# Encoder layer: the recurrence's levels on 64 by 64 blocks, and chain steps spread by their own lengths

## The chip, the cores and the metric

The kernel runs on one core of a Trainium2 chip. The core has five engines that work side by side: TensorE (PE in the profile, with its weight loads PEld), VectorE (DVE), ScalarE (ACT), GpSimd (POOL) and SyncE (SP, which issues most DMAs). The metric is the device time in microseconds (us) of one execution, as a median of several. A kernel is compared with another by that time; a profile is taken of one execution apart.

## The reference

One layer of an encoder is applied, with shared weights, to a batch of 512 tokens and a batch of 256 tokens, 1024 wide. Half of the 16 heads are dilated window attention; the other half are bidirectional HGRN2 heads, a gated linear recurrence. What the change touches is the part inside a chunk of 64 tokens:

```python
A = jnp.cumsum(gc, axis=-2)
diff = A[:, :, :, None, :] - A[:, :, None, :, :]
decay = jnp.exp(jnp.where(causal[:, :, None], diff, -jnp.inf))
att = jnp.einsum('bhtk,bhtsk,bhsk->bhts', qc, decay, kc)
o_intra = jnp.einsum('bhts,bhsv->bhtv', att, vc)
```

There is one scan forward and one backward, their outputs are added, normalised and gated, joined with the attention's output, and multiplied by an output weight. A gated feed-forward network with a short convolution follows.

## The kernel before

All 768 tokens are held in on-chip memory with the feature on the partitions. Float32 products of the projections are made as three products of rounded parts (`stationary_w`, L338). The first 25 weight tiles belong to the mixer's input projection. `tile_unit` takes such a tile through eight feature blocks `k`; each `k` is six matmuls of 512 and 256 columns, and each of these is one record in the trace.

**The chain.** For each of four pairs of heads, `chain(j)` computes the recurrence. Instead of a sum over tokens one by one, it builds the 128 by 128 matrix of weights between tokens in levels m = 1, 2, 4, 8, 16, 32, 64: at level m, key block and query block are neighbours of m tokens each. For each level a burst of small float32 matmuls multiplies keys by queries that carry the decay to that level's boundary. Then `update_q` (L409) and `update_k` (L397, L401, L403) multiply the decays of the next level in. Level 0 (the diagonal) and the levels 1 to 16 are computed on blocks of 32 by 32 (`small`, L430): 6 chunks, 4 blocks and 2 heads make 48 matmuls a burst. Level 0 is copied to a small array `cd`, and each level is laid over it under a mask (`copy_predicated`, L449), which is 1 where key and query differ by that level. Level 32 is a burst of 24 matmuls of 64 by 64 (L468), the two halves of the 128 by 128 matrix that lie off the diagonal another 24 (L477). Then follow transposes of the keys (L492), products of keys and values (L499), their combination (`comb`, L510), the output (L524, L527), the sums of squares (L534), the reciprocal root on GpSimd (L538), its spreading over 64 columns (L540), transposes of that (L544) and the gating (L546, L547).

**What sets the order.** The chain is a generator: each `yield` ends a step. `tile_unit` calls `pace(0.5)` after each `k`, so that a step of the chain is put in after every two `k` (12 records of L338). In the stretch of value tiles (`value_tile`, L346) after the fourth pair, `side(2)` puts in two steps after each of six tiles; what is left over goes into the tile unit behind. Each unit also splits the weight tile three ahead into its rounded part (ACT, L242) and the rest (DVE or POOL, L243). Within each engine instructions run in order. For TensorE, VectorE and ScalarE this order is laid out by a scheduler when the kernel is built; for SyncE and GpSimd it is the order of the code.

Of the kernel before, what the change touches and what calls it, by code (L numbers as in the profile page):

```python
# [19 lines left out]
NPAIR = 4  # L20
EPS = 1e-6
BRANCHES = ((128, 1), (512, 4), (2048, 16))
LEVELS = (1, 2, 4, 8, 16)
HALF = ((0, 64), (64, 128))


# [27 lines left out]
def const_arrays():  # L54


    c = np.zeros((128, N_CST), np.float32)
    c[:, C_IDENT:C_IDENT + 128] = np.eye(128)
    c[:64, C_ONES] = 1.0
    c[64:, C_ONES + 1] = 1.0  # L60
    tab = np.zeros((128, N_TAB), np.float32)
    p = np.arange(128)[:, None]
    delta = np.abs(p - (np.arange(896)[None, :] - 384))
    mult = np.zeros(delta.shape, np.float64)
    for window, dil in BRANCHES:
        mult += (delta % dil == 0) & (delta // dil <= window // (2 * dil))
    tab[:, :896] = np.where(mult > 0, 8.0 * np.log(np.maximum(mult, 1.0)), -1e30)
    inv = np.float32(500000.0) ** (-np.arange(8, dtype=np.float32) * np.float32(2.0) / np.float32(16))
    pos = np.concatenate([np.arange(SA), np.arange(SB)]).astype(np.float32)
    ang = (pos[None, :] * inv.astype(np.float32)[:, None]).astype(np.float32).astype(np.float64)  # L70
    for row in range(64):
        r = row % 16
        tab[row, 896:896 + T] = np.cos(ang[r % 8])
        tab[64 + row, 896:896 + T] = np.sin(ang[r % 8]) * (-1.0 if r < 8 else 1.0)
    s = np.arange(32)
    x = s[:, None] ^ s[None, :]
    m = np.zeros((128, len(LEVELS), 32), np.int32)
    for i, lv in enumerate(LEVELS):
        m[:, i] = np.tile((x >= lv) & (x < 2 * lv), (4, 1))
    return c, tab, m.reshape(128, -1)  # L80


# [10 lines left out]
class Encoder:  # L93
    def __init__(self, tc, a):
        self.tc, self.nc, self.a = tc, tc.nc, a
        self.pools = {}
        self.open("c", "left")
        self.cst = self.pools["c"][1].tile([128, N_CST], F32, name="cst")
        self.par = self.pools["c"][1].tile([128, NROWS], F32, name="par")
        self.sm = self.pools["c"][1].tile([128, 512], F32, name="sm")  # L100
        self.nsm = 0
        self.ident = self.cst[:, C_IDENT:C_IDENT + 128]
        self.W = self.ref("c", "W", 8192, True)
        self.RAW = self.ref("c", "RAW", 3072)
        self.V = self.ref("c", "V", 6144)
        self.open("x", "right")
        self.X = self.ref("x", "X", 12288, True)
        self.xh, self.xl = self.X, self.X + 6144
        self.open("s", "left")
        S0 = self.ref("s", "S0", 4608)  # L110
        self.open("u", "left")
        self.pm = self.pools["u"][1].tile([128, len(LEVELS), 32], I32, name="pm")
        S = self.S = self.ref("u", "S", 15488)
        n = 0

        def region(k):
            nonlocal n
            n += k
            return S + (n - k)

        self.sets = [(S0, S0 + 1536, S0 + 2304), (region(1536), region(768), region(768))]
        self.G = region(768)
        self.LQ = [S0]
        self.U = region(3072)
        self.KT = region(1024)
        self.Kb = region(768)
        self.ATT = region(1536)
        self.S1, self.S2 = region(768), region(768)
        self.TT = region(1536)
        self.CD = region(384)  # L130
        self.MZ = region(1024)
        self.SQ = region(768)
        self.psum = tc.tile_pool(name="ps", bufs=1, space=bass.MemoryType.PSUM)
        self.ps = self.psum.__enter__().tile([128, 8, 512], F32, name="ps")
# [111 lines left out]
    def prologue_loads(self):  # L246
# [29 lines left out]
        nc.sync.dma_start(self.pm, a["pmask"].rearrange("p (l s) -> p l s", s=32))  # L276
        yield

    def params(self):
# [135 lines left out]
    def chain(self, j):  # L415
# [7 lines left out]
        def small(kt, qv):  # L423
            b = 4 + 2 * par[0]
            par[0] ^= 1
            for c in range(NTT):
                for bk in range(4):
                    t0 = 128 * c + 32 * bk
                    for h in range(2):
                        nc.tensor.matmul(ps[32 * bk:32 * bk + 32, b + h, 32 * c:32 * c + 32], self.v(kt + t0, 32, *HALF[h]),  # L430
                                         qv(t0, h), start=True, stop=True)
            return ps[:, b:b + 2, 0:192].rearrange("p h (c s) -> p h c s", s=32)

        cd = self.v(self.CD, 384).rearrange("p (h c s) -> p h c s", h=2, s=32)
        ts = [(self.U, T)]
        for m in (1, 2, 4, 8, 16, 32, 64):
            ts.append((self.TT if m == 1 else ts[-1][0] + ts[-1][1] * 2, ts[-1][1] // 2))
        kb = [ka, self.Kb]
        s = small(kd, lambda t0, h: self.v(q + t0, 32, *HALF[h]))
        nc.scalar.activation(cd, s, AF.Copy)  # L440
        self.update_k(1, *ts[0], ka, kc, self.Kb)
        self.next_products(*ts[0], ts[1][0])
        yield

        def after(i, m, s=None):

            self.update_q(m, *ts[i], q2)
            if s is not None:
                nc.vector.copy_predicated(cd, self.pm[:, i][:, None, None, :].to_broadcast([128, 2, NTT, 32]), s)  # L449
            if m < 64:  # L450
                self.update_k(2 * m, *ts[i + 1], kb[(i + 1) % 2], kc, kb[i % 2])
                self.next_products(*ts[i + 1], ts[i + 2][0])

        for i, m in enumerate(LEVELS):
            after(i, m, small(kb[i % 2], lambda t0, h: self.q_view(q2, m, t0, 32, h)))
            yield


        def att(c, h, sb, tb):
            o = 128 * (c % 4) + 64 * tb  # L460
            return ps[64 * sb:64 * sb + 64, 4 + 2 * h + c // 4, o:o + 64]

        kt = kb[1]
        for c in range(NTT):
            for cb in range(2):
                t0 = 128 * c + 64 * cb
                for h in range(2):
                    nc.tensor.matmul(att(c, h, cb, cb), self.v(kt + t0, 64, *HALF[h]), self.q_view(q2, 32, t0, 64, h),  # L468
                                     start=True, stop=True)
        after(5, 32)  # L470
        yield
        kt = kb[0]
        for c in range(NTT):
            for cb in range(2):
                s0, t0 = 128 * c + 64 * cb, 128 * c + 64 * (1 - cb)
                for h in range(2):
                    nc.tensor.matmul(att(c, h, cb, 1 - cb), self.v(kt + s0, 64, *HALF[h]),  # L477
                                     self.v(q2 + T * (1 - cb) + t0, 64, *HALF[h]), start=True, stop=True)
        after(6, 64)
        kt = kb[1]  # L480
        t, nb = ts[7]
        for h in range(2):
            for b, n in ((0, SA), (1, SB)):
                nc.scalar.activation(self.v(self.ATT + T * h + SA * b, n), ps[:, 4 + 2 * h + b, 0:n], AF.Copy)
        am = self.v(self.ATT, 2 * T).rearrange("p (h c s) -> p h c s", h=2, s=128)
        for bk in range(4):
            nc.vector.tensor_copy(am[32 * bk:32 * bk + 32, :, :, 32 * bk:32 * bk + 32], cd[32 * bk:32 * bk + 32])
        yield

        src = [kt + 128 * c for c in range(6)] + [kc + 128, kc + 256]  # L490
# [4 lines left out]
        yield  # L495
        tok = [0, 1, 2, 3, 4, 5, 1, 2]
        for n in range(8):
            for h in range(2):
# [16 lines left out]
        comb(7, tb(2), 3, 7)  # L515
        comb(2, tf(2), 6, 2)
        comb(1, tb(1), 7, 1)
        yield
# [12 lines left out]
        yield  # L531
# [7 lines left out]
        yield  # L539
        nc.vector.tensor_copy(self.v(self.SQ, T).rearrange("p (n v) -> p n v", v=64), rs[:, :, None].to_broadcast([128, 12, 64]))  # L540
        yield
# [370 lines left out]
    def run(self):  # L912
# [8 lines left out]
        heavy, light = [], []  # L921

        def side(n=1):
            for _ in range(n):
                while heavy:
                    try:
                        next(heavy[0])
                        break
                    except StopIteration:
                        heavy.pop(0)  # L930

        def finish():
            while heavy:
# [11 lines left out]
        def pace(x):  # L945
            nonlocal due
            due += x
            while due >= 1:
                due -= 1
                side()  # L950


        self.prenorm_rows(0)
# [38 lines left out]
        for j in range(NPAIR):  # L992
# [3 lines left out]
                n += 1  # L996
            finish()
            heavy.append(self.chain(j))

        for i in range(NTT):  # L1000
            out = ps[:, (0, 2, 1, 3)[i % 4], 0:384]
# [232 lines left out]
```

## Time and profile before

| what | value |
|---|---|
| median of 3 runs | 1038.61 us (1038.47 to 1043.16) |
| profiled execution: its own time | 1039.73 us |
| profiled execution: span in the trace | 1037.9 us |
| granted TensorE clock, mean | 0.993 of full speed |
| TensorE busy | 997.8 us, 96% |
| VectorE busy | 641.5 us, 62% |
| ScalarE busy | 496.1 us, 48% |
| matmul records, weight-load records | 8239, 8239 |
| the chains' stretch of the program | about 90 to 310 us |

"Busy" is the time in which an engine has an instruction under way. An engine's idle time is put down to what ended it last: "DVE S L510" says that VectorE's line 510 released it; "issue" says that the engine waited for nothing that the profile shows. Each float32 matmul of the chain is two records of PE and two of PEld. In a row of the timeline, neighbouring instructions are merged, "x96" is their count, and the brackets tell the idle time before the row.

### The profile page before, as it was taken

To read this page: it belongs to the slowest core of one execution; us is meant where nothing else is said; L and a number is where in the kernel's file an instruction comes from. 1 tells how busy PE (TensorE), PEld (TensorE's weight loads), DVE (VectorE), ACT (ScalarE), POOL (GpSimd) and SP (SyncE) were. 2 spreads that over 40 slices of the span, in tenths; PEclk is the share of its full clock that TensorE was granted. 3 is DMA by queue.
4 is the path that set the end of the run, shared out by engine and by line. 5 is a ranking of instruction groups with operands and counts; after the bars stand their busy time and mean duration, and the time that the engine had idled before them with its cause. 6 is when DMAs were issued, how large, how long until landed. Compare 5 with 4: busy or idle time off the path is not lost.

```text
span 1037.9 us, 19821 instructions
## 1 busy us (share of the span) xinstructions
PE 997.8 (96%) x8239; PEld 889.0 (86%) x8239; DVE 641.5 (62%) x1110; ACT 496.1 (48%) x909; POOL 49.5 (5%) x45
## 2 busy tenths in 40 slices
PE   5998999989999999999989999999999999999997
PEld 5987788778878777679879999999999998888885
DVE  5445748375631776736799778877777773335334
ACT  4362526243232888854656555555445563334321
POOL 1100000000012101000100000000000000000001
PEclk9999999999999999999989999999999999999999
DMA  8041111111023221123335322333323376475413
GB/s 273 19 123 42 43 42 44 42 27 39 23 62 93 61 64 42 51 103 115 120 96 146 112 86 83 101 108 112 112 83 101 105 239 214 163 255 171 127 46 122
DMA packets 109883, 104.04 MB, mean 100 GB/s; under 512 B 4602, under 2 KB 89698, under 8 KB 109794
## 3 DMA queue, kind: packets, MB, share of 16 engines
q1 hardware_dynamic: 108930, 101.21, 31.9%
q8 instruction: 64, 1.05, 0.4%
q10 hardware_dynamic: 864, 1.57, 0.4%
q14 instruction: 25, 0.20, 0.1%
HBM read 85.46 MB, written 14.94 MB: 97 GB/s over the span
## 4 chain that ended last, share of the span: by engine, by line
PE 80%; issue 7%; DVE 6%; ACT 3%; DMA 1%; POOL 1%; SPq 0%; DVEq 0%; POOLq 0%; ACTq 0%
PE ps L857 31%; PE ps L1159 17%; PE ps L338 17%; PE ps L723 4%; PE ps L643 2%; PE ps L430 2%; PE ps L676 2%; PE ps L346 2%; PE ps L665 2%; PE ps L527 1%; DMA RAW<-w_in 1%; DVE S L412 1%; ACT W L242 1%; POOL sm L304 1%; PE ps L524 1%
## 5 line engine op out<-in xcount | busy, mean ns | idle before, releaser
L338 PE MATMUL ps<-X,W 128*128 128x512 f32 (+1 forms) x1200 | 230.4, 342 | 1.3 <-issue 1.3
L338 PEld LDWEIGHTS ps<-X,W 128*128 128x128 f32 x1200 | 185.1, 188 | 28.6 <-issue 3.8
L857 PE MATMUL ps<-XN,W 128*128 128x384 f32 x1056 | 191.7, 339 | 4.7 <-ACT XN L808 4.2
L857 PEld LDWEIGHTS ps<-XN,W 128*128 128x128 f32 x1056 | 186.5, 191 | 6.1 <-ACT XN L808 5.0
L1159 PE MATMUL ps<-W,XN 128*128 128x512 f32 x792 | 179.7, 389 | 0.0
L1159 PEld LDWEIGHTS ps<-W,XN 128*128 128x128 f32 x792 | 148.7, 188 | 30.8
L242 ACT ACTIVATE W<-RAW 128x1024 fp32r<-128x1024 f32 (+1 forms) x92 | 79.6, 868 | 179.5 <-PE ps L338 81.8
L857 PE MATMUL ps<-X,W 128*128 128x384 f32 x792 | 143.2, 338 | 0.0
L857 PEld LDWEIGHTS ps<-X,W 128*128 128x128 f32 x792 | 139.8, 188 | 0.0
L243 DVE TENSOR_TENSOR W<-RAW,W 128x512 fp32r<-128x512 f32 (+1 forms) x82 | 78.1, 955 | 74.6 <-ACT W L242 74.6
L242 ACT ACTIVATE W<-V 128x512 fp32r<-128x512 f32 x88 | 55.2, 629 | 58.6 <-PE ps L857 55.1
L243 DVE TENSOR_TENSOR W<-V,W 128x512 fp32r<-128x512 f32 x88 | 59.7, 687 | 17.8 <-ACT W L242 17.7
L346 PE MATMUL ps<-W,X 128*128 128x256 f32 (+1 forms) x432 | 66.5, 310 | 4.2 <-ACT X L817 2.7
L346 PEld LDWEIGHTS ps<-W,X 128*128 128x128 f32 x432 | 61.4, 194 | 5.9 <-ACT X L817 3.3
L243 DVE TENSOR_TENSOR XN<-X,XN 128x768 fp32r<-128x768 f32 x44 | 41.8, 955 | 35.8 <-ACT XN L242 35.8
L242 ACT ACTIVATE XN<-X 128x768 fp32r<-128x768 f32 x44 | 36.7, 839 | 42.8 <-PE ps L1159 42.1
L723 PE MATMUL ps<-W,X 128*128 128x512 f32 (+1 forms) x288 | 57.1, 343 | 0.0
L723 PEld LDWEIGHTS ps<-W,X 128*128 128x128 f32 x288 | 44.1, 189 | 6.8 <-issue 1.6
L242 ACT ACTIVATE W<-EX 128x512 fp32r<-128x512 f32 (+1 forms) x34 | 25.3, 744 | 46.8 <-PE ps L1159 22.5
L243 DVE TENSOR_TENSOR W<-EX,W 128x512 fp32r<-128x512 f32 (+1 forms) x34 | 28.2, 828 | 29.3 <-ACT W L242 29.3
L304 POOL TENSOR_TENSOR sm<-sm 128x1 f32<-128x1 f32 x24 | 15.2, 641 | 622.8 <-DVE sm L748 588.0
L397 ACT ACTIVATE S<-S 128x384 f32<-128x384 f32 x28 | 15.4, 549 | 46.9 <-PE ps L430 36.6
(187 smaller groups left out, 1159.6 us busy)
## 6 DMA issues: line engine op xcount, KB each, us to landing
X<-gd SPq DMA_DIRECT2D x44, 384.0 KB
RAW<-w_in SPq DMA_DIRECT2D x32, 512.0 KB
RAW<-w_gate SPq DMA_DIRECT2D x14, 512.0 KB
RAW<-w_up SPq DMA_DIRECT2D x13, 512.0 KB
RAW<-w_down SPq DMA_DIRECT2D x13, 512.0 KB
gd<-UM SPq DMA_DIRECT2D x22, 256.0 KB
EX<-w_up SPq DMA_DIRECT2D x9, 512.0 KB
EX<-w_down SPq DMA_DIRECT2D x9, 512.0 KB
```

The lines of the kernel that those rows point to most:

```text
L242: nc.scalar.activation(self.r(hi, n), self.v(src, n), AF.Copy)
L243: (eng or nc.vector).tensor_tensor(self.r(lo, n), self.v(src, n), self.v(hi, n), op=OP.subtract)
L304: self.nc.gpsimd.tensor_tensor(r, mean, self.mhalf, op=OP.pow)
L338: nc.tensor.matmul(out, self.r(wo + 128 * k, 128), self.r(xo + T * k + t0, tn), start=(k == 0 and first), stop=(k == NK - 1 and last))
L346: self.nc.tensor.matmul(out, self.r(xo + T * k + 128 * i, 128), self.rap(wo + 128 * k, [[1024, tiles], [1, 128]]), start=(k == 0 and first ...
L430: nc.tensor.matmul(ps[32 * bk:32 * bk + 32, b + h, 32 * c:32 * c + 32], self.v(kt + t0, 32, *HALF[h]), qv(t0, h), start=True, stop=True)
L643: nc.tensor.matmul(ps[:, 4 + h, 0:L], self.r(QS + T * h + t0 + 128 * i, 128), self.r(x + T * h + t0, L), start=z, stop=not z)
L665: nc.tensor.transpose(ps[:, 6 + h, 128 * kt:128 * kt + 128], ms(j, n, h)[:, 128 * kt:128 * kt + 128], self.ident)
L676: nc.tensor.matmul(o[64 * h:64 * h + 64], self.v(vb + 128 * kt + 64 * h, 64), self.v(pt(s, h) + L * kt, L), start=kt == 0, stop=kt == L // ...
L723: nc.tensor.matmul(out, self.r(mo + T * f + 128 * i, 128), rhs, start=(f == 0 and first), stop=(f == NK - 1 and last))
L857: nc.tensor.matmul(out, self.r(wo + 128 * k, 128), self.r(xo + H * k, H), start=kind in BEGINS and k == 0 and first, stop=k == 3 and last, ...
L1159: nc.tensor.matmul(ps[:, banks[half][i], :], self.r(go + 128 * i, 128), self.r(wo_, 512), start=(f == 0 and first), stop=(f == NF - 1 and ...
```

## The change

The levels 0 to 16 are computed on blocks of 64 keys by 64 queries: 24 matmuls a burst, each with 64 weights' columns and 64 columns streamed. Level 32 becomes the sixth level of the same loop, laid over `cd` by its mask, so `cd` and the mask double in width (`cd` from 384 to 768 columns, the mask from 160 to 384 int32 columns, all loaded from memory at the start). The two off-diagonal halves are written to the same compact layout. The attention matrix is then put together by two copies on ScalarE and two on VectorE instead of four and four.

Each step of the chain now yields a length, and `pace` takes that length off what is due, so that the following step comes sooner or later by it. The steps of the sums of squares and of the spreading are one step. `side(2)` in the value tiles still takes two steps, whatever their lengths. The chain has 13 steps, before 14.

```diff
-LEVELS = (1, 2, 4, 8, 16)
+LEVELS = (1, 2, 4, 8, 16, 32)
...
-        self.pm = self.pools["u"][1].tile([128, len(LEVELS), 32], I32, name="pm")
+        self.pm = self.pools["u"][1].tile([128, len(LEVELS), 64], I32, name="pm")
...
-                for bk in range(4):
-                    t0 = 128 * c + 32 * bk
+                for cb in range(2):
+                    t0 = 128 * c + 64 * cb
                     for h in range(2):
-                        nc.tensor.matmul(ps[32 * bk:32 * bk + 32, b + h, 32 * c:32 * c + 32], self.v(kt + t0, 32, *HALF[h]),
+                        nc.tensor.matmul(ps[64 * cb:64 * cb + 64, b + h, 64 * c:64 * c + 64], self.v(kt + t0, 64, *HALF[h]),
                                          qv(t0, h), start=True, stop=True)
...
-        s = small(kd, lambda t0, h: self.v(q + t0, 32, *HALF[h]))
+        s = small(kd, lambda t0, h: self.v(q + t0, 64, *HALF[h]))
         nc.scalar.activation(cd, s, AF.Copy)
         self.update_k(1, *ts[0], ka, kc, self.Kb)
         self.next_products(*ts[0], ts[1][0])
-        yield
+        yield 1.3
...
         for i, m in enumerate(LEVELS):
-            after(i, m, small(kb[i % 2], lambda t0, h: self.q_view(q2, m, t0, 32, h)))
-            yield
-
-
-        def att(c, h, sb, tb):
-            o = 128 * (c % 4) + 64 * tb
-            return ps[64 * sb:64 * sb + 64, 4 + 2 * h + c // 4, o:o + 64]
-
-        kt = kb[1]
-        for c in range(NTT):
-            for cb in range(2):
-                t0 = 128 * c + 64 * cb
-                for h in range(2):
-                    nc.tensor.matmul(att(c, h, cb, cb), self.v(kt + t0, 64, *HALF[h]), self.q_view(q2, 32, t0, 64, h),
-                                     start=True, stop=True)
-        after(5, 32)
-        yield
+            after(i, m, small(kb[i % 2], lambda t0, h: self.q_view(q2, m, t0, 64, h)))
+            yield 1.25
...
-        for h in range(2):
-            for b, n in ((0, SA), (1, SB)):
-                nc.scalar.activation(self.v(self.ATT + T * h + SA * b, n), ps[:, 4 + 2 * h + b, 0:n], AF.Copy)
         am = self.v(self.ATT, 2 * T).rearrange("p (h c s) -> p h c s", h=2, s=128)
-        for bk in range(4):
-            nc.vector.tensor_copy(am[32 * bk:32 * bk + 32, :, :, 32 * bk:32 * bk + 32], cd[32 * bk:32 * bk + 32])
-        yield
+        s = ps[:, b:b + 2, 0:64 * NTT].rearrange("p h (c s) -> p h c s", s=64)
+        for cb in range(2):
+            p0, p1 = HALF[cb]
+            nc.scalar.activation(am[p0:p1, :, :, 64 - p0:128 - p0], s[p0:p1], AF.Copy)
+            nc.vector.tensor_copy(am[p0:p1, :, :, p0:p1], cd[p0:p1])
+        yield 0.6
...
             while due >= 1:
-                due -= 1
-                side()
+                due -= side()
```

The lengths of the later steps are 1 (transposes), 1.2 (products and combination), 0.7 (output), 2.3 (sums of squares with the spreading) and 1 (the last).

The first place is VectorE in the first chain, at the levels 1, 2 and 4. L409 multiplies the queries, L449 lays the level over `cd`, L401 and L403 multiply the keys, L243 is the remainder of a weight tile's split. Before:

```order
L449 COPY_PREDICATED S<-pm,ps 128x384
L401 TENSOR_TENSOR S_71<-S 128x96x2 x2
L403 TENSOR_TENSOR S_71<-S 128x96x4
L409 TENSOR_TENSOR S_71<-S_71,S 128x192x2x2
L449 COPY_PREDICATED S<-pm,ps 128x384
L401 TENSOR_TENSOR S<-S_71,S 128x48x4 x2
L403 TENSOR_TENSOR S_71<-S_71,S 128x48x8
L243 TENSOR_TENSOR W<-RAW,W 128x1024
L409 TENSOR_TENSOR S_71<-S_71,S 128x96x2x4
```

And of the change:

```order
L449 COPY_PREDICATED S<-pm,ps 128x768
L401 TENSOR_TENSOR S_71<-S 128x96x2 x2
L403 TENSOR_TENSOR S_71<-S 128x96x4
L243 TENSOR_TENSOR W<-RAW,W 128x1024
L409 TENSOR_TENSOR S_71<-S_71,S 128x192x2x2
L449 COPY_PREDICATED S<-pm,ps 128x768
L401 TENSOR_TENSOR S<-S_71,S 128x48x4 x2
L403 TENSOR_TENSOR S_71<-S_71,S 128x48x8
```

The split's remainder now stands ahead of level 2's L409, where it stood ahead of level 4's.

The second place is TensorE at the end of the last chain, in the first tile unit behind the value tiles. L534 (L522 in the change) are the sums of squares, L544 (L531) the transposes that need the spread reciprocal roots. Before, with 20 records of L338 between them:

```order
L534 MATMUL ps<-cst,S 128x2 x4
L338 MATMUL ps<-X,W 128x256
L534 MATMUL ps<-cst,S 128x2 x2
L338 MATMUL ps<-X,W 128x512
...
L338 MATMUL ps<-X,W 128x256
L544 MATMUL ps<-cst,S 128x128 x6
```

And of the change, with 8:

```order
L522 MATMUL ps<-cst,S 128x2 x4
L338 MATMUL ps<-X,W 128x256
L522 MATMUL ps<-cst,S 128x2 x2
L338 MATMUL ps<-X,W 128x512
...
L338 MATMUL ps<-X,W 128x256
L531 MATMUL ps<-cst,S 128x128 x6
```

Twelve records of L338 have moved from ahead of these transposes to behind them.

The third place is VectorE at the end of the first chain, where the next chain's queries are made (L374, L376) and the old chain's output is gated (L546 and L547; L533 and L534 in the change). Before:

```order
L537 TENSOR_SCALAR sm<-ps 128x12
L540 COPY S<-sm 128x768
L243 TENSOR_TENSOR W<-RAW,W 128x1024
L374 TENSOR_TENSOR S<-ps,S 128x512
L374 TENSOR_TENSOR S<-ps,S 128x256
L376 TENSOR_TENSOR S<-S 128x1536
L546 TENSOR_TENSOR S<-ps,S 128x512
L546 TENSOR_TENSOR S<-ps,S 128x256
L547 TENSOR_TENSOR V<-ps,S 128x512
```

And of the change:

```order
L243 TENSOR_TENSOR W<-RAW,W 128x1024
L374 TENSOR_TENSOR S<-ps,S 128x512
L374 TENSOR_TENSOR S<-ps,S 128x256
L412 TENSOR_TENSOR S<-S 128x12
L376 TENSOR_TENSOR S<-S 128x1536
L525 TENSOR_SCALAR sm<-ps 128x12
L527 COPY S<-sm 128x768
L533 TENSOR_TENSOR S<-ps,S 128x512
L533 TENSOR_TENSOR S<-ps,S 128x256
```

The end of the old chain now comes after the next chain's queries. On TensorE its last transposes stand 12 records of L338 ahead of the next chain's first burst, where they stood 36 ahead.

## Rows read from the trace of the kernel before

**Rows 1.** Page, busy time of each engine, its share of the span, instructions.
```profile
PE 997.8 (96%) x8239; PEld 889.0 (86%) x8239; DVE 641.5 (62%) x1110; ACT 496.1 (48%) x909; POOL 49.5 (5%) x45
```

**Rows 2.** Chains' stretch: length, busy PE, PEld, DVE, ACT, POOL; clock; DMA share, GB/s.
```profile
90.00:310.00 220.00, 206.44 (x3830) 174.97 (x3830) 129.87 (x241) 79.52 (x155) 11.41 (x5) 1.00 0.15 40
```

**Rows 3.** Waits of PE, whole span: waiting line, releaser, us in total, times, longest.
```profile
PE ps L430 <- issue: 8.3, 7, 2.0
PE ps L544 <- DVE S L540: 1.7, 1, 1.7
PE ps L527 <- DVE S L510: 1.7, 3, 0.6
PE ps L499 <- ACT S L494: 0.5, 3, 0.2
```

**Rows 4.** Timeline of PE, first chain: start, us, instruction, count, idle before.
```profile
93.84 0.94 PE L430 MATMUL ps<-S 64*32 64x32 f32 x83
96.51 0.30 PE L430 MATMUL ps<-S 64*32 64x32 f32 x13 [1.72 <-issue]
96.74 2.35 PE L338 MATMUL ps<-X,W 128*128 128x512 f32 x12
99.02 1.02 PE L430 MATMUL ps<-S,S 64*32 64x32 f32 x96
99.97 1.31 PE L338 MATMUL ps<-X,W 128*128 128x512 f32 x6
102.59 1.21 PE L338 MATMUL ps<-X,W 128*128 128x512 f32 x6 [1.30 <-issue]
```

**Rows 5.** Sum over the eight idle stretches of PE put down to issue.
```profile
sum 9.64, PE 0.05 PEld 0.01 DVE 1.76 ACT 0.00 POOL 0.00; mean PE 0.01 PEld 0.00 DVE 0.22 ACT 0.00 POOL 0.00
```

**Rows 6.** Page, DMA: all packets; one queue's packets, MB, share of 16 engines.
```profile
DMA packets 109883, 104.04 MB, mean 100 GB/s; under 512 B 4602, under 2 KB 89698, under 8 KB 109794
...
q8 instruction: 64, 1.05, 0.4%
```

**Rows 7.** Lines by form: count, busy us, mean ns, idle before and its releasers.
```profile
L430 PE MATMUL ps<-S 64*32 64x32 f32 x1920 | 21.5, 202 | 6.3 <-issue 6.3
...
L430 PE MATMUL ps<-S,S 64*32 64x32 f32 x384 | 4.4, 200 | 2.0 <-issue 2.0
...
L477 PE MATMUL ps<-S 64*64 64x64 f32 x192 | 3.7, 222 | 0.0
```

**Rows 8.** Timeline of PE, second chain: level 1's burst and the chain's one gap.
```profile
151.48 1.06 PE L430 MATMUL ps<-S 64*32 64x32 f32 x96
...
166.14 0.26 PE L430 MATMUL ps<-S 64*32 64x32 f32 x5 [0.56 <-issue]
```

**Rows 9.** Timeline of DVE, first chain, split and level 4.
```profile
104.57 1.23 DVE L243 TENSOR_TENSOR W<-RAW,W 128x1024 fp32r<-128x1024 f32 x1 [2.05 <-ACT W L242]
105.71 0.95 DVE L409 TENSOR_TENSOR S<-S,S 128x768 f32<-128x768 f32 x1
106.58 0.60 DVE L449 COPY_PREDICATED S<-pm,ps 128x384 f32<-128x384 int32 x1
...
107.59 0.55 DVE L403 TENSOR_TENSOR S<-S 128x384 f32<-128x384 f32 x1
```

**Rows 10.** Timeline of PE, first chain, level 8's burst (its queries come from level 4's L409).
```profile
106.95 1.02 PE L430 MATMUL ps<-S,S 64*32 64x32 f32 x96
```

**Rows 11.** Timeline of PE, end of the last chain.
```profile
301.02 0.50 PE L534 MATMUL ps<-cst,S 128*128 128x2 f32 x4
301.38 3.75 PE L338 MATMUL ps<-X,W 128*128 128x512 f32 x20
306.87 0.88 PE L544 MATMUL ps<-cst,S 128*128 128x128 f32 x6 [1.74 <-DVE S L540]
```

**Rows 12.** Timeline of DVE, end of the last chain.
```profile
304.10 2.71 DVE L540 COPY S<-sm 128x768 f32<-128x768 f32 x1 [2.38 <-POOL sm L538]
...
308.50 1.01 DVE L547 TENSOR_TENSOR V<-ps,S 128x512 f32<-128x512 f32 x2
```

More of the change, by code (lines that the diff above doesn't have):

```diff
@@ L74, in const_arrays @@
         tab[64 + row, 896:896 + T] = np.sin(ang[r % 8]) * (-1.0 if r < 8 else 1.0)
-    s = np.arange(32)
+    s = np.arange(64)
     x = s[:, None] ^ s[None, :]
-    m = np.zeros((128, len(LEVELS), 32), np.int32)
+    m = np.zeros((128, len(LEVELS), 64), np.int32)
     for i, lv in enumerate(LEVELS):
-        m[:, i] = np.tile((x >= lv) & (x < 2 * lv), (4, 1))
+        m[:, i] = np.tile((x >= lv) & (x < 2 * lv), (2, 1))
     return c, tab, m.reshape(128, -1)
@@ L111, in __init__ @@
         self.open("u", "left")
-        self.pm = self.pools["u"][1].tile([128, len(LEVELS), 32], I32, name="pm")
-        S = self.S = self.ref("u", "S", 15488)
+        self.pm = self.pools["u"][1].tile([128, len(LEVELS), 64], I32, name="pm")
+        S = self.S = self.ref("u", "S", 15872)
         n = 0
@@ L129, in __init__ @@
         self.TT = region(1536)
-        self.CD = region(384)
+        self.CD = region(768)
         self.MZ = region(1024)
@@ L275, in prologue_loads @@
         nc.sync.dma_start(self.v(PR, 128, o, o + 3 * NF), a["conv_w"].rearrange("l w (k p) -> (l w k) p", p=128))
-        nc.sync.dma_start(self.pm, a["pmask"].rearrange("p (l s) -> p l s", s=32))
+        nc.sync.dma_start(self.pm, a["pmask"].rearrange("p (l s) -> p l s", s=64))
         yield
@@ L426, in small @@
             for c in range(NTT):
-                for bk in range(4):
-                    t0 = 128 * c + 32 * bk
+                for cb in range(2):
+                    t0 = 128 * c + 64 * cb
                     for h in range(2):
-                        nc.tensor.matmul(ps[32 * bk:32 * bk + 32, b + h, 32 * c:32 * c + 32], self.v(kt + t0, 32, *HALF[h]),
+                        nc.tensor.matmul(ps[64 * cb:64 * cb + 64, b + h, 64 * c:64 * c + 64], self.v(kt + t0, 64, *HALF[h]),
                                          qv(t0, h), start=True, stop=True)
-            return ps[:, b:b + 2, 0:192].rearrange("p h (c s) -> p h c s", s=32)
-        cd = self.v(self.CD, 384).rearrange("p (h c s) -> p h c s", h=2, s=32)
+            return ps[:, b:b + 2, 0:64 * NTT].rearrange("p h (c s) -> p h c s", s=64)
+        cd = self.v(self.CD, 768).rearrange("p (h c s) -> p h c s", h=2, s=64)
         ts = [(self.U, T)]
@@ L448, in after @@
             if s is not None:
-                nc.vector.copy_predicated(cd, self.pm[:, i][:, None, None, :].to_broadcast([128, 2, NTT, 32]), s)
+                nc.vector.copy_predicated(cd, self.pm[:, i][:, None, None, :].to_broadcast([128, 2, NTT, 64]), s)
             if m < 64:
@@ L454, in chain @@
         for i, m in enumerate(LEVELS):
-            after(i, m, small(kb[i % 2], lambda t0, h: self.q_view(q2, m, t0, 32, h)))
-            yield
-        def att(c, h, sb, tb):
-            o = 128 * (c % 4) + 64 * tb
-            return ps[64 * sb:64 * sb + 64, 4 + 2 * h + c // 4, o:o + 64]
-        kt = kb[1]
-        for c in range(NTT):
-            for cb in range(2):
-                t0 = 128 * c + 64 * cb
-                for h in range(2):
-                    nc.tensor.matmul(att(c, h, cb, cb), self.v(kt + t0, 64, *HALF[h]), self.q_view(q2, 32, t0, 64, h),
-                                     start=True, stop=True)
-        after(5, 32)
-        yield
+            after(i, m, small(kb[i % 2], lambda t0, h: self.q_view(q2, m, t0, 64, h)))
+            yield 1.25
+        b = 4 + 2 * par[0]
         kt = kb[0]
@@ L476, in chain @@
                 for h in range(2):
-                    nc.tensor.matmul(att(c, h, cb, 1 - cb), self.v(kt + s0, 64, *HALF[h]),
+                    nc.tensor.matmul(ps[64 * cb:64 * cb + 64, b + h, 64 * c:64 * c + 64], self.v(kt + s0, 64, *HALF[h]),
                                      self.v(q2 + T * (1 - cb) + t0, 64, *HALF[h]), start=True, stop=True)
@@ L494, in chain @@
             nc.scalar.activation(self.v(self.KT + 512 * b, 512), ps[:, 4 + b, :], AF.Copy)
-        yield
+        yield 1
         tok = [0, 1, 2, 3, 4, 5, 1, 2]
@@ L517, in chain @@
         comb(1, tb(1), 7, 1)
-        yield
+        yield 1.2
         inter = [[(0, 1)], [(1, 0), (0, 7)], [(0, 3), (1, 6)], [(1, 2)], [(0, 5)], [(1, 4)]]
@@ L530, in chain @@
         nc.scalar.activation(self.v(self.SQ + SA, SB), o[1], AF.Square)
-        yield
+        yield 0.7
         ss = ps[:, 6, 0:12]
@@ L538, in chain @@
         nc.gpsimd.tensor_tensor(rs, ms, self.mhalf.to_broadcast([128, 12]), op=OP.pow)
-        yield
         nc.vector.tensor_copy(self.v(self.SQ, T).rearrange("p (n v) -> p n v", v=64), rs[:, :, None].to_broadcast([128, 12, 64]))
-        yield
+        yield 2.3
         rb = [ps[:, 7, :], ps[:, 6, 0:256]]
@@ L923, in side @@
         def side(n=1):
+            d = None
             for _ in range(n):
@@ L926, in side @@
                     try:
-                        next(heavy[0])
+                        d = next(heavy[0])
                         break
@@ L930, in side @@
                         heavy.pop(0)
+            return d or 1
         def finish():
@@ L998, in run @@
             heavy.append(self.chain(j))
+            due = 0.0
         for i in range(NTT):
```

## The prediction

> **What bounds the kernel now.** I read the busy shares first: TensorE is busy for 96% of the span, VectorE 62%, ScalarE 48% [rows 1]. So a term counts if it shortens TensorE's work or its idle time, and VectorE's and ScalarE's work counts only where TensorE waits for it. Then I cut the span by stage. In the chains' stretch, 220.00 us long, TensorE is busy 206.44 us, so 13.6 us are idle there, while VectorE works 129.87 us and ScalarE 79.52 us [rows 2]. The change acts here alone; behind this stretch the order of every engine's instructions stays as it was. The granted clock is full in it [rows 2], so it is no term.
>
> The list of TensorE's waits says what the 13.6 us are. The largest is L430, the bursts of 32 by 32, 8.3 us in 7 waits put down to "issue", which means that no semaphore is seen to hold the engine. Beside it stand 1.7 us of L527 for VectorE's combination, 1.7 us of L544 for the spreading and 0.5 us of L499 for ScalarE [rows 3]. With one more "issue" gap just behind a burst, in L338 [rows 4], the issue gaps are eight stretches, 9.64 us together, in which TensorE runs nothing [rows 5].
>
> What are these gaps? In the timeline of the first chain the reader is to count. Between the start of the record row at 96.51, which ends one gap, and the next gap at 101.28, TensorE runs 13 + 12 + 96 + 6 = 127 matmul records [rows 4]. Each has a weight load beside it, so this is 254 instructions. Now the whole program: 8239 matmuls and 8239 weight loads [rows 1] came in 64 packets of a queue of the kind "instruction", 1.05 MB [rows 6], which is 257 instructions and 16.4 KB a packet. So the gaps lie one packet of instructions apart: TensorE has run out of code. In a 32 by 32 stretch it uses 2 x 108 instructions in 3.2 us (one burst and 12 records of L338, 96.74 to 99.97), a packet in 3.8 us. In the stretches with 24 matmuls a burst, a packet lasts twice as long, and L477's matmuls have no idle time ahead of them [rows 7].
>
> The Trainium skill (Runtime: NRT & Kernel Launch, section "Instruction fetch mechanics") says that code comes in blocks of 256 instructions, fetched while the block before is run, and that crossing a boundary is "mostly hidden". This trace agrees in the block, by the 257 above, and not in the hiding, by the 9.64 us. By the rule the gaps would have another cause and stay, which is the first rival below.
>
> **The change part by part.**
>
> Stalls for code. A burst has 48 records of matmul where it had 96; in a chain, 288 records fall away, 1152 in all. The level stretch takes 48 + 15 records, twice, in one burst of about 0.9 us and 15 records of L338 at 0.19 us, so a packet lasts some 7.5 us instead of 3.8. I take 1.2 us of the 9.64 to stay, one gap of the kind seen: -8.4 us. Bounds: 0, if the gaps are not the code, and -9.6.
>
> Shorter bursts. The 24 bursts of L430 are busy 21.5 + 4.4 = 25.9 us, 1.08 us each; four bursts of 64 by 64 in L477 are busy 3.7 us, 0.93 us each [rows 7]. So half as many matmuls with twice the columns take 0.15 us less: 24 x 0.15 = -3.6 us. Level 32 and the off-diagonal bursts are of this form already and stay. What the trace does not show is 64 columns read in runs of 1 to 16 elements, as the levels 1 to 16 read their queries. For 32 columns the worst case, level 1, is drawn with 1.06 us [rows 8] and level 2 with 1.02 [rows 4], both under the mean of 1.08, so I charge nothing for the pattern. Bounds: -3.6, and twice the pass, 0.93 more on each of 20 bursts, +18.6, which is a rival.
>
> The Trainium skill (TensorEngine Tiling (Array Packing), section "Tiling Modes") gives eight independent tiles for 64 rows by 32 columns and four for 64 by 64. By that count a burst of half as many matmuls with twice the columns on half as many tiles would take twice as long. The 0.93 against 1.08 us says otherwise for this shape, so the tiles are not what sets the pace here; the time by the rule is that of the slow bursts below.
>
> Steps spread. The 192 records of L338 in a chain stay the same. Between products and output there are now 18 of them, before 12, so the combination gets 1.1 us more cover; the waits of L527 were 0.6 us at the longest [rows 3], so 1.7 us go. Of the 0.5 us of L499, whose distance stays 12, I take 0.3 to go, as the cross blocks now leave by two ScalarE instructions instead of four. Together -2.0 us; bounds -2.2 and 0.
>
> End of the last chain. Here the lengths do not help: the value tiles take two steps each, and one step less brings the transposes 12 records earlier. Before, 20 records (3.75 us) covered the way from the sums of squares over GpSimd and the 2.71 us copy, and 1.74 us were still idle [rows 11, 12]. Eight records cover 12 x 0.187 = 2.25 us less: +2.25 us. Nothing takes it back, as the copy and what comes before it start at the same point of the program. Bounds: +0.7, if the copy took 1.2 us, twice the masked copy of half its width [rows 9], and +2.25.
>
> VectorE. The masked copy of 384 columns took 0.60 us [rows 9]; 768 columns cost between 0.60 and 1.2, and I take 1.0. A level on VectorE ran from 105.71 to 108.14, 2.4 us [rows 9], and becomes 2.8 us. TensorE's period is 3.2 us with 12 records of L338 between bursts and 4.3 us with 18, so the level fits behind it. It is close in two places. First, the split now stands ahead of level 2's L409, and the next burst is 12 records later. The same pattern was there before at level 4: split from 104.57, L409 done at 106.66, burst at 106.95 [rows 9, 10], 0.29 us to spare. The burst in between is 0.09 to 0.15 us shorter now, so 0.15 to 0.2 us are left; what queues behind the split are that L409 and the level's other updates, and the next burst waits for L409. Second, a new chain's first burst writes the banks which the old chain's L547 reads. From the transposes to the end of L547 it took 306.87 to 309.51 = 2.64 us [rows 11, 12]; the new cover is the transposes and 12 records, 0.88 + 2.25 = 3.1 us at most, before 36 records. I charge 0.8 us for five such crossings. Bounds: 0 and +7.2, which is 0.3 us on each of 24 bursts.
>
> ScalarE's larger copy of level 0 and the two half-width copies are hidden: it works 79.52 of 220 us [rows 2], and no burst waits for them directly. The mask load grows from 80 to 192 KB in the prologue; at the mean of 100 GB/s [rows 6] that is 1.1 us of transfers at most, in a queue with weight tiles behind it, and I take +0.3.
>
> Sum: -8.4 - 3.6 - 2.0 + 2.25 + 0.8 + 0.3 = -10.65 us. From the profiled execution's 1039.73 us (span 1037.9 and 1.8 around it) this gives 1029.1. The median before lies 1.1 us lower, at 1038.61, so I predict **1028.0 us**.
>
> **The rivals.**
>
> The stalls stay. If the fetch is late because of the weight transfers that go at the same time and not because of the rate, or if the gaps are something else that the profile does not see, fewer instructions do little. For it: the second chain has the same rate and one gap of only 0.56 us [rows 8], so rate alone is not the cause. Against it: spacing by packets, and none in the 64 by 64 stretches of four chains. All of them staying gives 1028.0 + 8.4 = 1036.4 us, half of them 1031.6.
>
> VectorE becomes the bound of the levels. If a masked copy from the accumulation banks under a broadcast mask costs more than twice the old one, or the scheduler's order makes a split wait, each of 24 bursts starts some 0.3 us late: 7.2 us, 6.4 over my 0.8, which makes 1034.4 us. Against it: 129.87 of 220 us busy.
>
> The wide bursts read slowly (the other side). With short runs a 64-column burst could need its pass twice, 1.86 us. It is at the levels 1 to 16, 5 x 4 = 20 bursts; price 20 x 0.93 = 18.6 us, so 1046.6 us. It makes the kernel slower than before from 10.6 / 20 = 0.53 us a burst. Against it are level 1's burst in 1.06 us [rows 8] and level 2's in 1.02 [rows 4], where runs of 1 and of 2 cost nothing that can be seen.
>
> **How the numbers follow.** A measurement of this kernel can tell about 0.5%, 5.2 us, from no change: faster is under 1033.4, slower over 1043.8. The forecast has a chance of 0.70, with 1025.0 (all gaps, all waits gone, no new ones) to 1033 as its own range. Stalls staying, 0.16, a third of it on the fast side of 1033.4. VectorE the bound, 0.08, mostly within 0.5%, a quarter faster. Slow bursts, 0.04, slower. The last 0.02 is for what I do not see, slower or same. That is faster 0.77, same 0.18, slower 0.05. The range is from 1024.0 to 1036.0: it takes in the stalls' bound but for its end and VectorE's case, and leaves the slow bursts out.
>
> **What would show it.** Right: bursts of x48 at 0.93 us at all levels; the "instruction" queue at some 55 packets; the issue waits of the bursts down to 2 us or less; L527's counterpart without waits; the last transposes with some 4 us of idle time ahead of them; and 220 us of stage in about 209. Wrong: issue gaps still one packet apart and over 1 us long; bursts of the low levels longer than those of level 32; TensorE idle for L409 or L449 at each level. A change in time behind the chains' stretch would also prove me wrong, since I expect none there.

## The result and the profile after

The changed kernel takes **1028.52 us** (median of 4, 1027.96 to 1028.98); before took 1039.25 beside it. The ratio is 0.9889, 95% interval [0.9863, 0.9915]. Predicted were 1028.0 us. The profiled execution took 1028.98 us with a span of 1027.2.

The page's busy line, and its row of the "instruction" queue (packets, MB, share of 16 engines), answer to [rows 1, 6]:

```profile
PE 996.8 (97%) x7087; PEld 888.9 (87%) x7087; DVE 651.8 (63%) x1106; ACT 498.3 (49%) x901; POOL 49.4 (5%) x45
...
q8 instruction: 55, 0.90, 0.4%
```

Read TensorE's two numbers together: 1152 records are gone, and 9 packets of code, but only 1.0 us of busy time. So of the span's 10.7 us, 9.7 are idle time. (The busy time holds two terms of opposite sign, shorter bursts and matmuls at a slow clock; both come below.) Of TensorE's waits in the chains' stretch [rows 3], this is what the list still shows:

```profile
PE ps L531 <- DVE S L527: 3.8, 1, 3.8
```

The waits of L430 for issue, of L527 for the combination (L515 in the changed kernel) and of L499 for ScalarE (L487) have no row left. All 28 bursts of L430, level 32 now among them, start right behind what stands ahead of them. Here are level 1 and level 2 of the first chain in TensorE's timeline (start, us, count; compare [rows 4]):

```profile
94.39 1.23 PE L430 MATMUL ps<-S 64*64 64x64 f32 x48
95.55 3.43 PE L338 MATMUL ps<-X,W 128*128 128x512 f32 x18
98.91 0.97 PE L430 MATMUL ps<-S,S 64*64 64x64 f32 x48
99.80 2.37 PE L338 MATMUL ps<-X,W 128*128 128x512 f32 x12
102.10 0.93 PE L430 MATMUL ps<-S 64*64 64x64 f32 x48
```

Level 1's burst takes 95.55 - 94.39 = 1.16 us, level 2's 0.89. The masked copy and the place where the split stands ahead of level 2's L409, in VectorE's timeline (answering to [rows 9]):

```profile
99.76 1.23 DVE L243 TENSOR_TENSOR W<-RAW,W 128x1024 fp32r<-128x1024 f32 x1 [0.54 <-ACT W L242]
100.90 0.95 DVE L409 TENSOR_TENSOR S<-S,S 128x768 f32<-128x768 f32 x1
101.77 1.05 DVE L449 COPY_PREDICATED S<-pm,ps 128x768 f32<-128x768 int32 x1
```

L409 is done at 101.85 and the burst that needs it starts at 102.10: 0.25 us to spare, and no wait. The other close place is the second chain's first burst, which has to come behind the old chain's last gating (VectorE's timeline, then TensorE's):

```profile
140.70 1.01 DVE L534 TENSOR_TENSOR V<-ps,S 128x512 f32<-128x512 f32 x2
```

```profile
141.95 0.93 PE L430 MATMUL ps<-S 64*64 64x64 f32 x48
```

The gating ends at 141.71, 0.24 us ahead of the burst, and TensorE has no idle time there.

The one place that got worse is the last chain's end [rows 11]. First TensorE's timeline, then a window (length, busy PE, PEld, DVE, ACT, POOL, granted clock, DMA share, GB/s):

```profile
286.35 1.64 PE L338 MATMUL ps<-X,W 128*128 128x512 f32 x8
291.81 1.54 PE L531 MATMUL ps<-cst,S 128*128 128x128 f32 x6 [3.82 <-DVE S L527]
```

```profile
290.90:297.40 6.50, 5.59 (x19) 4.94 (x20) 2.81 (x5) 0.00 (x0) 0.44 (x1) 0.50 0.28 81
```

The idle time grew from 1.74 to 3.82 us, and at its end and behind it the granted clock is 0.50, the level of 1.2 GHz, for 6.5 us. The transposes are drawn with 1.54 us where they took 0.88, and the L338 behind them runs slowly too. The prediction had the first part and not the second.

### The profile page after: what moved, and what is told of

Read it like the earlier page. It is cut to its first block, busy times and chain, and to the rows that moved or that the text cites. A ratio compares the mean times of both kernels' runs of the same rounds, so it can differ in the third digit from the quotient of the medians.

```text
span 1027.2 us, 17503 instructions
## 1 busy us (share of the span) xinstructions
PE 996.8 (97%) x7087; PEld 888.9 (87%) x7087; DVE 651.8 (63%) x1106; ACT 498.3 (49%) x901; POOL 49.4 (5%) x45
## 4 chain that ended last, share of the span: by engine, by line
PE 86%; issue 6%; DVE 3%; ACT 2%; POOL 1%; DMA 1%; SPq 0%; DVEq 0%; POOLq 0%; ACTq 0%
PE ps L844 31%; PE ps L338 19%; PE ps L1149 17%; PE ps L710 4%; PE ps L346 4%; PE ps L430 2%; PE ps L630 2%; PE ps L663 2%; PE ps L652 2%; PE ps L515 1%; DMA RAW<-w_in 1%; PE ps L512 1%; DVE XN L796 1%; DVE V L747 0%; POOL sm L526 0%
## 5 line engine op out<-in xcount | busy, mean ns | idle before, releaser
L338 PE MATMUL ps<-X,W 128*128 128x512 f32 (+1 forms) x1200 | 232.5, 345 | 0.0
L338 PEld LDWEIGHTS ps<-X,W 128*128 128x128 f32 x1200 | 187.2, 190 | 28.0 <-issue 2.4
L243 DVE TENSOR_TENSOR W<-RAW,W 128x512 fp32r<-128x512 f32 (+1 forms) x82 | 78.1, 955 | 66.0 <-ACT W L242 65.9
L243 DVE TENSOR_TENSOR W<-V,W 128x512 fp32r<-128x512 f32 x88 | 59.8, 688 | 17.8 <-ACT W L242 17.7
L243 DVE TENSOR_TENSOR XN<-X,XN 128x768 fp32r<-128x768 f32 x44 | 41.8, 955 | 35.8 <-ACT XN L242 35.7
L243 DVE TENSOR_TENSOR W<-EX,W 128x512 fp32r<-128x512 f32 (+1 forms) x34 | 28.2, 830 | 29.6 <-ACT W L242 29.6
L860 ACT ACTIVATE V<-ps 128x384 f32<-128x384 f32 x66 | 31.4, 475 | 6.3 <-PE ps L844 6.3
```

The lines of the kernel that those rows point to most:

```text
L243: (eng or nc.vector).tensor_tensor(self.r(lo, n), self.v(src, n), self.v(hi, n), op=OP.subtract)
L338: nc.tensor.matmul(out, self.r(wo + 128 * k, 128), self.r(xo + T * k + t0, tn), start=(k == 0 and first), stop=(k == NK - 1 and last))
L860: self.nc.scalar.activation(self.v(o, H), self.ps[:, self.pair_banks(p)[BANK_OF[kind]], 0:H], AF.Copy)
```

## The experiments

The theory: TensorE ran out of code, because stretches with 32 by 32 bursts use up a packet of instructions faster than the next one comes. The rivals: the spreading of the steps, not the blocks, removed the gaps; or the gaps belong to the small tiles and have nothing to do with code. The second question is what the end of the last chain costs. Medians in us, and ratios to the kernel before on the same chip:

| run | time | ratio, 95% interval | issue gaps in the chains' bursts |
|---|---|---|---|
| e1 blocks only | 1027.95 | 0.9886 [0.9873, 0.9900] | none |
| e2 spread only | 1033.05 | 0.9934 [0.9921, 0.9946] | 1.9 us in 3 |
| e3 blocks, even, filled | 1049.37, one run | | 1.2 us in 3 |
| e4 end covered | 1022.62 | 0.9834 [0.9821, 0.9847] | none |
| e5 filled twice | 1087.31, one run | | 7.7 us in 10 |
| e6 level 1 contiguous | 1027.78, one run | | none |
| e7 end half covered | 1024.33 | 0.9827 [0.9810, 0.9844] | none |
| e8 even, end covered | 1025.12 | 0.9833 [0.9816, 0.9850] | none |
| e9 changed, again | 1028.59 | 0.9873 [0.9848, 0.9898] | none |
| e10 as e4, again | 1022.12 | 0.9811 [0.9782, 0.9841] | none |
| e11 as e8, again | 1025.96 | 0.9848 [0.9821, 0.9875] | none |
| e12 before, again | 1041.12, one run | | 9.0 us in 7 |

**e1, the blocks alone.** Every length is taken out, and the spreading copy is a step of its own again:

```diff
-            yield 1.25
+            yield
...
+        yield
         nc.vector.tensor_copy(self.v(self.SQ, T).rearrange("p (n v) -> p n v", v=64), rs[:, :, None].to_broadcast([128, 12, 64]))
-        yield 2.3
+        yield
```

> The 64 by 64 blocks with the even steps of before (14 steps of length 1). Theory (the stalls come from the number of instructions in a stretch, and the blocks alone halve it): no issue gap of a packet's kind in the bursts, the combination's waits of about 1.7 us back, 1.7 us idle ahead of the last transposes and no fall of the clock there; 1024 to 1027 us, so faster than the changed kernel by 2 to 4 us. Rival (the spreading removes the stalls): gaps of 4 us or more stay, 1031 us or more. Second rival (VectorE cannot keep up with 12 records between bursts): no issue gaps, but TensorE waits for L409 or L449 for 3 us or more in all, 1028 to 1032 us.

No issue gap, and no wait of a burst for VectorE, even with 12 records between all bursts. So the blocks suffice, and the second rival falls. The time is 1 us above the range I gave, and only 0.6 us under the changed kernel's where I gave 2 to 4. Still, the blocks alone are no slower than the whole change: what the lengths save in waits, they lose again at the last chain's end. The waits are as expected:

```profile
PE ps L532 <- DVE S L528: 1.7, 1, 1.7
PE ps L515 <- DVE S L498: 1.7, 3, 0.6
...
PE ps L487 <- ACT S L482: 0.8, 3, 0.3
```

**e2, the spreading alone.** The lengths are put on the kernel before, with its 32 by 32 blocks:

```diff
-            yield
+            yield 1.25
```

> The 32 by 32 blocks with the lengths given to the steps. Theory: a packet lasts 4.4 us instead of 3.8, so only a part of the stalls goes, 3 to 7 us stay; the combination's waits go, the end of the last chain loses 4 to 5 us as in the changed kernel; 1034 to 1039 us. Rival (the spreading removes the stalls): under 1 us of gaps, 1031 to 1033 us.

The gaps fall from 9.64 to 1.9 us, with the number of instructions as before (64 packets of code):

```profile
101.97 0.26 PE L430 MATMUL ps<-S,S 64*32 64x32 f32 x6 [1.22 <-issue]
...
260.40 0.74 PE L430 MATMUL ps<-S 64*32 64x32 f32 x63 [0.39 <-issue]
...
267.93 0.33 PE L430 MATMUL ps<-S 64*32 64x32 f32 x25 [0.29 <-issue]
```

Neither expectation holds in its size. A few more records between bursts remove four fifths of the gaps. Of what is left, only the first gap lies in the three chains that the lengths spread; the other two lie among the value tiles of the fourth, which take two steps each whatever the lengths are. Either half of the change would have taken most of them, so the two gains do not add.

**e3 and e5, the instructions put back.** e3 is e1 with 24 added matmuls of 2 columns behind each burst of the levels, whose results nothing reads; e5 has 48:

```diff
+            for c in range(NTT):
+                for cb in range(2):
+                    t0 = 128 * c + 64 * cb
+                    for h in range(2):
+                        nc.tensor.matmul(ps[64 * cb:64 * cb + 64, b + h, 400 + 2 * c:402 + 2 * c], self.v(kt + t0, 64, *HALF[h]),
+                                         self.v(kt + t0, 2, *HALF[h]), start=True, stop=True)
```

> The 64 by 64 blocks with even steps, and behind each burst of the levels 24 matmuls of 2 columns that nothing reads, so that a burst has 96 records again as before the change. Theory: issue gaps come back, one packet of 256 instructions apart, 4 to 10 us in all, and the instruction queue has some 64 packets again. Rival (the gaps belong to the 32-column tiles, not to the number of instructions): no gaps over 0.5 us; the time grows only by the added matmuls.

> The 64 by 64 blocks with even steps and 48 added matmuls of 2 columns behind each burst, so that 312 instructions go in about 4.6 us, a packet in 3.8 us as before the change. In the first runs a packet lasted 7.5 us (no gaps), 4.5 us (1.2 us of gaps, one added set), 4.4 us (1.9 us, spread 32 by 32 blocks) and 3.8 us (9.6 us, the kernel before). Theory (the time for which a packet lasts sets the gaps): 6 us of gaps or more, a packet apart. Rival (the small 32-column tiles or the even steps with them make the gaps): about twice the 1.2 us of one set at most.

With 64 by 64 blocks the gaps are back (66 and 76 packets of code): 1.2 us with one set, less than the 4 us I expected, and with two sets 3.5 + 2.0 + 1.6 + 0.6 = 7.7 us:

```profile
PE ps L442 <- issue: 3.5, 4, 1.5
...
PE ps L430 <- issue: 2.0, 3, 0.8
...
PE ps L436 <- issue: 1.6, 2, 1.0
...
PE ps L477 <- issue: 0.6, 1, 0.6
```

The time for which a packet lasts is read from two bursts that follow each other, here in e1 and then in e5:

```profile
100.19 0.93 PE L430 MATMUL ps<-S 64*64 64x64 f32 x48
...
103.35 0.93 PE L430 MATMUL ps<-S,S 64*64 64x64 f32 x48
```

```profile
108.12 0.98 PE L430 MATMUL ps<-S 64*64 64x64 f32 x48
...
112.68 0.93 PE L430 MATMUL ps<-S,S 64*64 64x64 f32 x48
```

In e1 there are 60 records, so 120 instructions, in 3.16 us: 256 last 6.7 us. In e5 there are 312 instructions in 4.56 us: 256 last 3.7 us. In the same way e3 has 216 in 3.80 us (104.07 to 107.87), so 4.5 us, and e2 has 444 over two bursts in 7.70 us (156.69 to 164.39), so 4.4 us.

e3's and e5's times hold the added matmuls, and in e5 a clock that fell behind some of its gaps; only the gaps are read here.

Set side by side: 3.8 us gave 9.6 us of gaps (before), 3.7 gave 7.7 (e5), 4.4 gave 1.9 (e2), 4.5 gave 1.2 (e3), and 6.7 (e1) and 7.5 (the changed kernel) gave none. Form of tile, number of packets and spacing differ between these runs; the time for which a packet lasts separates those with many gaps from those with few and none. That is what I call shown. Not shown is why only some ends of packets have a gap: in the first chain of before, 255 records, two packets, lie between the second gap and the third, and the second chain, at the same rate, has one gap.

**e12, the kernel before, a second trace.**

> The kernel before once more, for a second trace. Its runs lie between 1038.5 and 1044.5 us, those of the changed kernel within 1.1 us of each other. Theory (the stalls for code are made by a race of the fetch with the engine, and so vary): issue gaps again a packet apart, but in other places and with another sum, anywhere from 8 to 15 us. Rival (something fixed in the program makes them): the same eight places and 9.6 us within 0.5 us.

Seven gaps, 9.0 us, end at the same instructions as seven of the eight before (13, 63, 5, 24, 5, 74 and 24 records left in the burst), but they have other lengths: the second chain's gap, 0.56 us at 166.14 [rows 8], is now 1.86. So the program fixes the places and not the lengths; of the theory the "other places" were wrong, of the rival the same lengths. The eighth gap, 1.30 us at 102.59 [rows 4], is missing. Ahead of its place TensorE ran at a slow clock in this trace (timeline, then a window):

```profile
96.95 3.54 PE L338 MATMUL ps<-X,W 128*128 128x512 f32 x12
100.43 1.15 PE L430 MATMUL ps<-S,S 64*32 64x32 f32 x96
101.51 2.36 PE L338 MATMUL ps<-X,W 128*128 128x512 f32 x12
```

```profile
99.50:101.00 1.50, 1.50 (x62) 1.06 (x63) 0.63 (x2) 0.00 (x0) 0.00 (x0) 0.50 0.05 11
```

The twelve records of L338 took 3.54 us where they took 2.35 [rows 4]: this packet lasted 1.2 us longer, and no gap came behind it. With the same instructions, in this pair of traces, the slower engine stalls less, as the theory says. The third chain shows the same, where this trace also shows what a gap can draw after it:

```profile
208.83 0.37 PE L430 MATMUL ps<-S 64*32 64x32 f32 x24 [1.64 <-issue]
209.12 3.13 PE L338 MATMUL ps<-X,W 128*128 128x512 f32 x12
212.19 1.17 PE L430 MATMUL ps<-S,S 64*32 64x32 f32 x91
214.67 0.26 PE L430 MATMUL ps<-S,S 64*32 64x32 f32 x5 [1.31 <-issue]
```

```profile
210.30:213.40 3.10, 3.06 (x99) 2.30 (x98) 2.05 (x5) 0.00 (x0) 0.00 (x0) 0.52 0.02 5
```

Behind a gap of 1.64 us the granted clock is 0.52, and twelve records of L338 take 3.13 us where they took 2.35 [rows 4]. The gap one packet later is 1.31 us; in the first trace, with the full clock there, it was 2.01. Runs of before ranged from 1037.9 to 1045.3 us on this chip, those of the changed kernel from 1027.2 to 1029.4. Gaps of changing length, with a fall of the clock behind some, fit this; I traced two executions and not the slowest ones, so what makes the times vary is not shown.

**e4, e7, e8: the last chain's end.** One line behind the value tiles delays the chain's last step: -2 (e4) puts 32 records of L338 ahead of the last transposes in place of 8, -1 (e7) puts 20 there, as before the change. In e8, with even steps, -1 gives 32:

```diff
+        due = -2.0
```

> The changed kernel, with what is due set to -2 behind the value tiles, so that 32 instead of 8 records of L338 stand between the last sums of squares and the last transposes. Theory (3.8 us idle there and, because of it, a granted clock of 0.5 for some 6 us): no idle time and no fall of the clock, 1021.5 to 1023 us, 6 us under the changed kernel. Rival (the fall of the clock has another cause): 1024.5 to 1025.5 us, with the fall still there. Second rival (the output queue or the attention behind it is late instead): no gain.

> The changed kernel with what is due set to -1 behind the value tiles: 20 records of L338 between the last sums of squares and the last transposes, as before the change. Theory (idle time of 1.7 us leaves the granted clock alone, of 3.8 us does not): 1.7 us idle, no fall, 1024 to 1025 us. Rival (the fall comes from something else in the changed kernel): the fall stays, 1026 to 1027 us.

> The 64 by 64 blocks with even steps, and what is due set to -1 behind the value tiles, so that 32 records of L338 cover the last chain's end. Against the run of the same end with spread steps (1022.6 us) it tells what the spreading is worth by itself. Theory: 1.7 us of waits for the combination and 0.8 us for the products stay, so 1025 to 1026.5 us. Rival (the spreading is worth nothing): 1022 to 1023 us.

In e4 the wait is gone from the list, and so is the fall of the clock:

```profile
284.00:300.00 16.00, 16.00 (x102) 14.09 (x101) 4.86 (x6) 2.23 (x5) 7.02 (x3) 1.00 0.35 97
```

In e7 the wait is as before the change, 1.74 us, and the window that covers its L338 has the full clock, 2.4 GHz:

```profile
286.18 3.74 PE L338 MATMUL ps<-X,W 128*128 128x512 f32 x20
291.67 0.87 PE L531 MATMUL ps<-cst,S 128*128 128x128 f32 x6 [1.74 <-DVE S L527]
```

```profile
291.70:297.40 5.70, 5.70 (x35) 5.09 (x36) 1.95 (x4) 0.96 (x1) 0.00 (x0) 1.00 0.32 92
```

The span of e7 is 1022.5 us, 4.7 under the changed kernel's: 3.82 - 1.74 = 2.1 us of idle time, and the other 2.6 us are what the slow clock cost in that trace. (From the start of the last transposes to the attention's first matmul, L630, the changed kernel takes 41.60 us and e7 36.87; 2.1 of that are the 12 records that moved there, and the rest is 2.6.)

**e9, e10, e11: the same three on one chip.**

> The changed kernel once more, on one chip with the two versions of the last chain's end, which were timed in separate calls. Expected 1027.5 to 1029.5 us, as in its first runs, with 3.8 us of idle time at the last transposes and a fall of the clock behind it.

> Spread steps with 32 records at the last chain's end. If the end costs what its idle time and clock say (3.8 us and some 2.5 us): 5.5 to 6.5 us under the changed kernel on the same chip.

> Even steps with 32 records at the last chain's end. If the spreading is worth its waits (1.7 and 0.8 us): 2 to 3 us above the spread version on the same chip. If the spreading is worth nothing: within 0.7 us of it.

The three take 1028.59, 1022.12 and 1025.96 us. Covering the end is worth 6.5 us by these medians, and the spreading by itself 3.8 us, more than the 1.7 + 0.8 us of waits which it removes. The traces show where the rest lies. The attention's first matmul starts, in e10 and then in e11, at

```profile
327.67 0.40 PE L630 MATMUL ps<-QK 128*128 128x512 f32 x1
```

```profile
330.18 0.40 PE L631 MATMUL ps<-QK 128*128 128x512 f32 x1
```

The first bursts start at 91.12 and 90.81, so the stretch of the chains takes 236.55 and 239.37 us, and in e9, from 90.29 to 332.45, 242.16: covering the end is worth 5.6 us there and the spreading 2.8 (e4 and e8 differ by 2.8 us in this stretch too). Behind it, where the order of the instructions is the same, the traces of e9, e10 and e11 take 694.8, 692.9 and 694.6 us. That part of the differences does not come from the steps. e9's clock fell again, for a shorter time:

```profile
291.00:298.00 7.00, 6.08 (x28) 5.34 (x29) 2.81 (x5) 0.00 (x0) 0.45 (x1) 0.76 0.26 75
```

A mean of 0.76 over 7.0 us is 3.4 us at 0.50. e10 is the fastest version: 1022.1 us, 0.9811 of before.

**e6, level 1 read in one run.** Level 1's queries are 64 neighbouring columns of one plane, so this kernel leaves out the second plane at level 1, and its result is not the reference's:

```diff
+        if m == 1:
+            return self.v(q2 + t0, n, *HALF[h])
```

> The changed kernel with level 1's queries read as 64 neighbouring columns of one plane and not as the interleaving of two, so level 1 is not the reference's. Level 1's burst takes 1.16 us in the changed kernel (94.39 to 95.55), the others 0.86 to 0.90. Theory (the short runs cost 0.3 us): 0.86 us, some 1.2 us less in all. Rival (it is the place in the order, the first burst behind the copy of level 0): 1.16 us as before.

```profile
94.60 0.93 PE L432 MATMUL ps<-S 64*64 64x64 f32 x48
95.46 3.42 PE L338 MATMUL ps<-X,W 128*128 128x512 f32 x18
```

The burst takes 95.46 - 94.60 = 0.86 us, as the theory says: reading columns one by one from two planes in turn costs 0.3 us. Whether the change of plane or the single columns cost it, this run does not tell, as it takes both away. Level 2, with pairs of columns, costs 0.03.

## Why the prediction was right

It was right in the mechanism of the two large terms, the code and the blocks. That the total came within 0.5 us is in part luck: single terms missed by up to 2.4 us, in opposite directions.

- Stalls for code, -8.4: all 9.64 us went. I kept 1.2 us, which e1 and the changed kernel do not show.
- Shorter bursts, -3.6: 24 bursts of 1.08 and four of level 32 at about 0.93 were 29.6 us, 28 bursts are now 21.5 + 5.6 = 27.1, so -2.5 (the lines stand below). What I charged nothing for, the runs of one element, took back 0.3 us in each chain (e6).
- Combination and products, -2.0: both rows are gone, -2.2. With even steps (e1) they are there.
- End of the last chain, +2.25: the idle time grew by 2.1, and the clock added 2.6 (e7), so +4.7. The step that failed is the sentence "The granted clock is full in it [rows 2], so it is no term", and with it the bound of +2.25: I took the clock of the kernel before for that of the changed one, and priced idle time by its length alone.
- VectorE, +0.8: no wait; at the two places that I called close, VectorE is done 0.25 and 0.24 us ahead of the burst. The masked copy costs 1.05 us where I took 1.0.
- The mask's load, +0.3: not to be seen; the first burst starts at 90.18 us, in the kernel before at 90.62.

The bursts of the changed kernel by form:

```profile
L430 PE MATMUL ps<-S 64*64 64x64 f32 x1056 | 21.5, 228 | 0.0
...
L430 PE MATMUL ps<-S,S 64*64 64x64 f32 x288 | 5.6, 223 | 0.0
```

Measured terms: -9.6 - 2.5 - 2.2 + 4.7 = -9.6 of the span's -10.7 us. Where the attention's first matmul starts, before and in the changed kernel, tells where the rest lies:

```profile
343.74 0.40 PE L643 MATMUL ps<-QK 128*128 128x512 f32 x1
```

```profile
333.41 0.40 PE L630 MATMUL ps<-QK 128*128 128x512 f32 x1
```

From the first burst to there it is 253.12 and 243.23 us, -9.9, so 0.3 us of the stretch are not assigned. 0.4 us lie ahead of the first burst and 0.4 us behind the stretch, where I expected no change; traces with the same order there differ by up to 1.8 us (e9, e10), so this need not come from the change.

The rival "the stalls stay" falls by e1, e2 and e5 together. The Trainium skill's sentence (Runtime: NRT & Kernel Launch, "Instruction fetch mechanics") that crossing a block is "mostly hidden" agrees with e1 and the changed kernel, at 6.7 and 7.5 us a packet without a gap, and not with before, at 3.8 us and 9.6 us of gaps. "VectorE becomes the bound" falls by the empty list of waits, in e1 even with 12 records between bursts. The "slow bursts" are real for level 1 alone, at 0.3 us instead of 0.93.

The rival had a chance of 0.16, in part because weight transfers might make the fetch late. No run here took the transfers away, so whether they delay single fetches, and why the second chain had only one gap, stays open.

## What to carry to other kernels

Count instructions per microsecond where matmuls are small: an idle TensorE put down to "issue", in gaps one packet of 256 instructions or two apart, points to a shortage of code. Here fewer and larger instructions removed it, and the same ones spread among long ones removed most of it. When steps are spread or merged, follow the last one by hand, where the long work runs out: 12 records that moved there cost 4.7 us, where the whole change gained 10.7. Time each half of a change alone: with that end uncovered the lengths gained nothing, as e1 shows. Price an idle stretch of TensorE by the clock behind it as well as by its length.

## What was not expected of the hardware

- Behind 3.82 us of idle time the granted clock was 0.50 for 6.5 us (the changed kernel) or 3.4 us (e9); behind a gap of 1.64 us it was 0.52 over 3.1 us (e12); behind 1.74 us ahead of the last transposes it stayed at 1.00 (e7), and also behind the gap of 2.01 us in the kernel before. Length alone does not decide.
- A burst of 64 by 64 whose streamed columns alternate between two places one by one took 1.16 us, with neighbouring columns 0.86 (e6). In the kernel before, with 32 columns and twice the instructions, level 1 was drawn with 1.06 us and level 2 with 1.02.
- A packet that lasted 1.2 us longer, at a slow clock, had no gap behind it where the same instructions had 1.30 us at the full clock (e12 against before).
